# The last merge in two token passes with seven block products for eight, and its sums and output weights made ahead

## The chip, the core and the metric

The kernel runs on one core of one Trainium2 chip. The metric is the device time of one execution in microseconds (us). The engines are TensorE (PE: matrix products; PEld is its weight load), VectorE (DVE), ScalarE (ACT), GpSimd (POOL) and SyncE (SP, here an issuer of DMA transfers). All run side by side and meet through semaphores.

## The reference, cut to what matters

One step of a backbone layer for 2048 sample tokens and 128 prompt tokens, width 1024. Behind an adaptive RMSNorm one projection gives everything else:

```python
proj = einsum('btd,de->bte', xn, w_in)
qkv, beta, dec, z_a, u_b, v_b, z_b, x_c, z_c, gates = split(proj, points)
...                                  # three branches: DeltaNet scan, spatial gating, Fourier
br = stack([o_a, o_b, o_c], axis=2)                        # 3 branches, 512 wide
pb = einsum('btnw,nwd->btnd', br, w_branch)                # to 1024 channels each
gt = sigmoid(gates.reshape(B, T, 3, D_MODEL))              # 3 gates of 1024 channels
merged = einsum('btnd,btnd->btd', gt, pb)
out = einsum('btd,de->bte', merged, w_out)                 # then gated residual and RMSNorm
```

The gates are the largest product: 3072 of the projection's columns over all 2176 tokens.

## The kernel before, in words

**Numbers.** Every fp32 operand is kept as a pair of fp16 tiles, high part and low part, behind a power of two as scale. A product is then three matmuls for each 128 rows of depth: high by high, high by low, low by high. All go through the helper `mm` at L250, so the profile has one PE line. Depth 1024 takes 24 matmuls, depth 512 takes 12. The normed input lies in SBUF as `xh` and `xl` (1024 channels in 8 rows of tiles, by 2176 tokens). It stays until the gates are done. Weights arrive in fp32 (`wst`), are squared on ScalarE to find a scale (L315), and are turned into `whi` on ScalarE (L327) and `wlo` on VectorE (L328). For branch weights the names are `bst`/`wst`, `bhi` and `blo`.

**Order of stages.** Norm and small projections come first. Then q, k, v follow in 12 blocks of 128 channels (L927 to L956). Each block runs on PE over five token tiles (four of 512, one of 128). ScalarE moves each tile from PSUM to `raw` (L944), VectorE does the three-tap convolution over `raw` (L947 to L949), ScalarE and GpSimd the SiLU (L952, L953), and GpSimd stores the block (L954). `raw` has two buffers. Beside it a generator `decays()` computes the decay tables of the scan on VectorE and ScalarE, a few instructions for each token tile. After that come the rest of the projection, the branches and the scan.

**Merges.** `merge(n)` (from L1702) does one branch n: for each of 8 output blocks `db` and each token tile it makes the gate product (24 matmuls), a sigmoid on ScalarE (L1733), the branch product (12 matmuls), a multiplication on VectorE (L1742), and an addition on GpSimd into `mrow` (L1743). `mrow` is loaded from and stored to the DRAM rows `mD` (named `mrg`; L1717, L1758). The order is branch 1, 2, 0. In a merge's last block the next branch is loaded (`st` from `br`) and turned into the fp16 tile `big` (L1699, L1700). Weights of the next block are loaded and converted a block ahead (`weight_step`).

**Output weights and token sums of the output stage.** Merge 0 is the last. In its first four blocks it also makes the output weights (`out_w`: pairs `wohi`/`wolo` in SBUF, and four weight sums to DRAM as `tD`, named `tw`). In blocks 4 to 7 it adds, for each token tile, the four-way sums of merged rows that the output product takes (`quarters`, L1878 to L1887), and GpSimd stores them in DRAM as `paD` (named `pa`).

**Output stage.** It multiplies two token tiles at a time with seven block products where plain blocking takes eight (`two_tiles`; 84 matmuls of 512 columns each time, eight times). It starts with `prompt_left` (24 matmuls). Its inputs come through SP in one fixed order: rows of the prompt, `pa` of the first pair, weight sums `tw`, input rows, `pa` of the second pair. The large tiles of this stage lie on memory that has been used: `xh` and `xl` carry the input rows (`room`), the first pair's sums (`own`) and two of the weight sums; the others lie in a pool `opa` opened after `ms_.close()`.

**Who orders the work.** The code is written by stage, and a tile scheduler orders the instructions on each engine. Each engine then executes in that order. A tile that takes memory of a closed pool waits for the last users of what lay there.

## Time and profile before

| | |
|---|---|
| runs: median (lowest to highest), 3 runs | 2144.0 us (2141.62 to 2144.39) |
| profiled execution: span from first to last instruction | 2142.8 us |
| q, k, v blocks | about 145 to 422 us |
| merges 1, 2 and 0 | about 1050 to 1975 us |
| of these merge 0, the last | 1707.8 to 1975.1 us |
| output stage | 1975.1 us to the end |

The profiled execution's own time is its span; what a run has around it is not recorded apart, and the span lies 1.2 us under the median of the runs. In the profile's rows "L250" is the line of the program, "b<-xh,whi" says that PSUM bank b is written from the tiles xh and whi, "128x512" is the moving tile, and "x4" says that four like instructions are merged in one row. In a timeline the last part in brackets is the idle time of the engine before the row and what ended it. "SPq" and "POOLq" are rows in which SP or GpSimd issues a DMA.

### The profile page before, as it was taken

The page shows a single profiled execution, that of the slowest core. Times are in us where ns is not written, and L with a number is a line of the kernel's source. Part 1 is how long each engine was busy: PE and PEld are TensorE (multiplying, and loading weights), DVE is VectorE, ACT ScalarE, POOL GpSimd, SP SyncE. Part 2 cuts the span into 40 slices and gives each one's busy share as a digit, 9 for nine tenths or more (in the row PEclk, how much of TensorE's full clock was granted, in tenths as well). Part 3 has the DMA queues.
Part 4 walks back from the last instruction along what each step waited for, and adds up shares of the span by engine and source line. Part 5 has one row for each costly group of instructions (what it writes and reads, how often), then busy time and mean ns, then how long its engine had stood idle before and what let it go on. Part 6 is the DMA issues. An engine that isn't in the chain of part 4 may idle for free.

```text
span 2142.8 us, 42632 instructions
## 1 busy us (share of the span) xinstructions
PE 2084.4 (97%) x16133; PEld 1197.6 (56%) x16133; DVE 1330.7 (62%) x2945; ACT 1060.6 (49%) x2456; POOL 843.1 (39%) x1089
## 2 busy tenths in 40 slices
PE   8999999999999999999899999999999999999998
PEld 4454444455555677777555556565655444444443
DVE  6656854378777786566655555866665564666245
ACT  5554744465656664445544445665654353443112
POOL 0321332225565554552322233355543234343464
PEclk9999999999999999999999999999999999999999
DMA  9625722177877743444665556867664645456862
GB/s 352 222 78 191 266 103 103 62 222 234 262 226 240 228 143 99 121 132 141 204 182 166 164 160 188 262 211 226 211 198 128 210 169 173 167 197 234 344 221 89
DMA packets 222766, 403.25 MB, mean 188 GB/s; under 512 B 39704, under 2 KB 109616, under 8 KB 219744
## 3 DMA queue, kind: packets, MB, share of 16 engines
q1 hardware_dynamic: 167520, 290.58, 42.5%
q0 software_dynamic: 15216, 65.89, 8.2%
q10 hardware_dynamic: 39824, 44.05, 6.0%
q8 instruction: 127, 2.08, 0.4%
q14 instruction: 79, 0.65, 0.1%
HBM read 258.19 MB, written 142.24 MB: 187 GB/s over the span
## 4 chain that ended last, share of the span: by engine, by line
PE 50%; DVE 8%; DMA 7%; POOL 3%; ACT 3%; issue 3%; SPq 1%; ACTq 0%; POOLq 0%; DVEq 0%
PE b L250 49%; DMA st<-br 3%; POOL E L1115 1%; DMA pa<-pa 1%; DVE XB L1114 1%; POOL st L1466 1%; DVE big L1700 1%; DMA ei<-XB 1%; ACT big L1699 1%; ACT nd L1066 0%; DVE n L1083 0%; POOL ss L1024 0%; DVE XB L1123 0%; DMA br<-st 0%; DMA skn<-kv 0%
## 5 line engine op out<-in xcount | busy, mean ns | idle before, releaser
L250 PE MATMUL b<-xh,whi 128*128 128x512 f16 (+1 forms) x1920 | 650.3, 347 | 2.9 <-DVE sg L1456 1.8
L250 PE MATMUL b<-xl,whi 128*128 128x512 f16 (+1 forms) x1920 | 650.6, 347 | 0.0
L250 PE MATMUL b<-xh,wlo 128*128 128x512 f16 (+1 forms) x1920 | 649.7, 347 | 0.0
L250 PEld LDWEIGHTS <-whi 128*128 128x128 f16 x3856 | 352.4, 98 | 326.1 <-issue 6.9
L250 PEld LDWEIGHTS <-wlo 128*128 128x128 f16 x1928 | 188.6, 98 | 175.6 <-issue 1.2
L250 PE MATMUL b<-big,bhi 128*128 128x512 f16 (+1 forms) x960 | 253.2, 348 | 2.8 <-ACT big L1699 1.5
L250 PE MATMUL b<-big,blo 128*128 128x512 f16 (+1 forms) x480 | 163.4, 347 | 0.0
L1743 POOL TENSOR_TENSOR mrow<-mrow,sg 128x512 f32<-128x512 f32 (+1 forms) x80 | 94.4, 1183 | 129.4 <-DVE sg L1742 98.6
L953 POOL TENSOR_TENSOR cy<-cy,raw 128x545 f32<-128x545 f32 (+1 forms) x48 | 64.5, 1372 | 182.1 <-ACT raw L952 182.1
L250 PEld LDWEIGHTS <-xh 128*128 128x128 f16 x1496 | 117.1, 98 | 28.7 <-issue 1.3
L250 PEld LDWEIGHTS <-bhi 128*128 128x128 f16 x960 | 87.8, 98 | 79.2 <-issue 4.0
L1115 POOL TENSOR_TENSOR E<-E,XB 128x31 f32<-128x31 f32 (+15 forms) x155 | 94.3, 608 | 83.8 <-DVE XB L1114 67.6
L250 PEld LDWEIGHTS <-xl 128*128 128x128 f16 x1068 | 98.1, 98 | 44.8 <-DMA tw<-tw 1.3
L1733 ACT ACTIVATE sg<-b,winv 128x512 f32<-128x512 f32 (+1 forms) x120 | 74.0, 616 | 86.3 <-PE b L250 85.5
L1188 POOL COPY T<-ES 32x256 f16<-32x256 f16 x68 | 30.0, 442 | 182.9 <-DMA ES<-ei 159.6
L250 PE MATMUL b<-whi,xh 128*128 128x128 f16 x544 | 92.8, 219 | 0.0
L250 PE MATMUL b<-whi,xl 128*128 128x128 f16 x544 | 92.8, 219 | 0.0
L250 PE MATMUL b<-wlo,xh 128*128 128x128 f16 x544 | 92.8, 219 | 0.0
L328 DVE SCALAR_TENSOR_TENSOR wlo<-wst,wsc,whi 128x1024 f16<-128x1024 f32 x52 | 69.9, 1345 | 31.8 <-ACT whi L327 30.5
L315 ACT ACTIVATE wlo<-wst 128x1024 f16<-128x1024 f32 x52 | 54.9, 1055 | 53.0 <-DMA wst<-in_w_blk_dram 50.3
L1295 POOL TENSOR_TENSOR skn<-skn,ed 128x512 f32<-128x512 f32 x34 | 37.0, 1089 | 110.5 <-DMA skn<-kv 110.5
L1114 DVE TENSOR_TENSOR XB<-XB,E 128x31 f32<-128x31 f32 (+15 forms) x155 | 54.3, 350 | 42.0 <-POOL E L1115 41.3
(531 smaller groups left out, 4328.9 us busy)
## 6 DMA issues: line engine op xcount, KB each, us to landing
wst<-in_w_blk_dram SPq DMA_DIRECT2D x58, 512.0 KB, 4.5
pa<-pa POOLq DMA_DIRECT2D x16, 896.0 KB, 4.6
qkv<-cy POOLq DMA_DIRECT2D x12, 1089.0 KB, 5.3
st<-br SPq DMA_DIRECT2D x48, 256.0 KB, 3.3
mrow<-mrg SPq DMA_DIRECT2D x16, 576.0 KB, 4.7
pa<-pa SPq DMA_DIRECT2D x5, 1792.0 KB, 17.1
dc<-dec SPq DMA_DIRECT2D x17, 512.0 KB, 4.6
kq<-qkv SPq DMA_DIRECT2D x34, 256.0 KB, 4.3
```

The costliest lines, as they stand in the source:

```text
L250: newest[0] = PE.matmul(out, l, r, start=start, stop=stop, skip_group_check=reopened)
L315: w.squared = A.activation(w.lo, st, AF.Square, accum_out=ss)
L328: w.low = V.scalar_tensor_tensor(w.lo, st, s, w.hi, ALU.mult, ALU.subtract)
L953: G.tensor_tensor(y[:, c0:c1], y[:, c0:c1], raw[:, 1 + c0:1 + c1], ALU.mult)
L1114: V.tensor_tensor(t3, X3[:, 0:k, k:k + 1].to_broadcast([P, k, n_]), E3[:, k:k + 1, k:32].to_broadcast([P, k, n_]), ALU.mult)
L1115: G.tensor_tensor(E3[:, 0:k, k:32], E3[:, 0:k, k:32], t3, ALU.subtract)
L1188: G.tensor_copy(T16[rows(a0, b), :, :, b], ES[0:32, :, 2 * a0 + b, :, wT])
L1295: G.tensor_tensor(h3(kn_), h3(kn_), bc(ed[:, d, t, :], P), ALU.mult)
L1466: G.tensor_tensor(o, sg, src, ALU.mult)
L1699: A.activation(o16[:, 0, g, t0:t0 + tn], st, AF.Copy, scale=s)
L1733: gated_[0] = A.activation(sg, ps, AF.Sigmoid, scale=gw.inv)
L1743: G.tensor_tensor(mr, mr, sg, ALU.add)
```

## The change

**Seven products.** The last merge no longer goes through `merge`. `last_merge` takes a pair of gate blocks (i and i + 4), and cuts the tokens and the depth in halves a and b: tokens 0 to 511 with 512 to 1023, and so on (`QUADS`). Of the 2 by 2 by 2 small products it makes seven, on sums of token halves and sums of weight quarters, in place of eight. It runs over order (pass 1 with blocks 0 to 3, then pass 0): pass 1 takes tokens 1024 to 2047 and the 128 prompt tokens (as a small quad of 64 and 64), pass 0 tokens 0 to 1023. Branch products stay as many as before. The weights of each pair are loaded, added and converted in both passes (`pair_weights`); the scales of the first pass are kept.

**Sums ahead.** The sums of token halves (`token_sums`) and the output weights (`out_w`) are made as a generator `beside`, three steps behind each 512-token tile of q, k, v from block 1 on: 132 steps, just as many as there are places for. Results go to DRAM (`sD`, `woD`, `tD`). At the last block of merge 2 the sums are loaded again: three of the four into tiles `ts` of a new pool `last`, the fourth over the second token halves of `xh`/`xl`. After pass 1 the output weights are loaded into columns 1024 to 2047 of `xh`/`xl`, and the prompt's merged rows into the last 128 columns.

**Memory.** `mrow` and its neighbour `bwp` get a pool of their own (`mr_`) that is closed behind merge 2; a pool `orp` is opened on this memory with the new tiles of the last merge (`wt2`, `bst`, `bhi`, `blo`, `mr`, `pm`, `pa`, `sums`). The tiles of the output stage (`room`, three `pa`, `gpr`, `xr`) are moved to `opa`, opened behind `ms_.close()` and `last_s.close()`, on memory of `big`, `orp` and `last`. All four `tw` now go to columns 0 to 1023 of `xh`/`xl`.

**Small things.** `gates` (the rows of the residual gate) are advanced in every block of merge 2 and finished there; `dynamic_dma_scratch_size` is set to 4096.

Around the start of the last merge, PE before: behind the last product of merge 2 (bank b_23145) and two short sums stands the first gate product of merge 0 (b_23228), with weights made a block earlier.

```order
L250 MATMUL b_23145<-big_13436,blo_22675 128x128
L250 LDWEIGHTS ones_2_89
L250 MATMUL b_23201<-bsums_2759_23199,ones_2_89 128x27
L250 MATMUL b_23220<-sg_22571,sel_106 2x256 x2
L250 LDWEIGHTS whi_22891
L250 MATMUL b_23228<-xh_94,whi_22891 128x512
L250 LDWEIGHTS whi_22891
L250 MATMUL b_23228<-xl_95,whi_22891 128x512
```

The same place on PE after. The first row is again merge 2's last product.

```order
L251 MATMUL b_23758<-big_14010,blo_23330 128x128
L251 LDWEIGHTS ones_2_89
L251 MATMUL b_23817<-bsums_2925_23815,ones_2_89 128x27
L251 LDWEIGHTS ones_2_89
L251 MATMUL b_23847<-wscb_23845,ones_2_89 128x1
L251 LDWEIGHTS bhi_23873
L251 MATMUL b_24045<-big_14010,bhi_23873 128x512
L251 LDWEIGHTS bhi_23873
L251 MATMUL b_24045<-big_14010,bhi_23873 128x512
```

Where gate products with finished weights stood, there is now the sum for the scale of the first pair's weights (`wscb`), and behind it a branch product whose weights `bhi_23873` come of `bst`.

ScalarE there, after: `big` is the next branch's tile, and the rows L1987 are the squares of the first pair's weights, written to `wt` (the tile `wt2` of pool `orp`).

```order
L1785 ACTIVATE big_14010<-st_23729,bsc_23500 128x512
L1987 ACTIVATE wt_2933_23841,wss_2934_23842<-wst_23834 128x1024
L1785 ACTIVATE big_14010<-st_23775,bsc_23500 128x512
L1785 ACTIVATE big_14010<-st_23783,bsc_23500 128x128
L1987 ACTIVATE wt_2933_23841,wss_2934_23842<-wst_23835 128x1024
L1785 ACTIVATE big_14010<-st_23785,bsc_23500 128x128
L934 ACTIVATE bhi_23873<-bst_23838,bscale_23827 128x512
L934 ACTIVATE bhi_23877<-bst_23838,bscale_23827 128x512
L934 ACTIVATE whi_23853<-wst_23834,gscale_23832 128x512
```

The first of the rows L1987 waits for the last store of `mrow` to `mrg` in merge 2, since `wt2` lies where `mrow` lay; so does SP's load of `bst_23838`.

SP at the start of the output stage, before: `xh` and `xl` take the prompt's rows, the first pair and two weight sums.

```order
L1965 DMA xh_94<-in_x_prompt_dram 128x512
L1965 DMA xl_95<-pa 128x4x1792
L1965 DMA xl_95<-tw 128x4096 x2
L1965 DMA tw_3065_25690<-tw 128x4096
L1965 DMA xh_94<-in_x_sample_dram 128x1024 x2
L1965 DMA tw_3065_25690<-tw 128x4096
L1965 DMA pa_25703<-pa 128x4x1792
```

And after:

```order
L2162 DMA sg_26259<-gate 128x512
L2182 DMA room_26274<-in_x_prompt_dram 128x512
L2182 DMA pa_3208_26283<-pa 128x4x1792
L2182 DMA xh_94<-tw 128x4x1024 x2
L2182 DMA xl_95<-tw 128x4x1024
L2182 DMA room_26274<-in_x_sample_dram 128x1024 x2
L2182 DMA xl_95<-tw 128x4x1024
L2182 DMA pa_3209_26291<-pa 128x4x1792
```

The transfers and their order are nearly the same. The first waited for PE's last read of `xh` and `xl`. Now `room` waits for the last store of sums to `pa`, since it lies on memory of pool `orp`, and the rest is queued behind it.

The diff, cut to its core (the bodies of `token_sums`, `out_w` and `pair_weights` are shortened):

```diff
+QUADS = [(0, 512, 512, 0), (1024, 1536, 512, 512), (2048, 2112, 64, 1024)]
...
     for i, (n_, g) in enumerate(_blocks()):
+        if n_ == C_G:
+            break
...
+    def token_sums():
+        for p_, (a0, b0, cn, _) in enumerate(QUADS):
+            a, b = slice(a0, a0 + cn), slice(b0, b0 + cn)
+            for k in range(4):
+                f11, f12, f21, f22 = [sb(ep, [P, cn], "sg", bufs=4) for _ in range(4)]
+                for on, f, kk, ts in ((G, f21, k, b), (V, f11, k, a), (G, f22, k + 4, b), (G, f12, k + 4, a)):
+                    on.tensor_tensor(f, xh[:, kk, ts], xl[:, kk, ts], ALU.add)
...
+                for i, f in enumerate((f22, f11, f21, f12)):
+                    st = sb(ep, [P, 2, cn], "st", F16, bufs=3)
+                    as_pair(st[:, 0], st[:, 1], f, 1.0)
+                    SY.dma_start(sD[p_][:, i, :, k, :], st)
+                    yield 1
...
+                if tn == 512 and ct:
+                    for _ in range(3):
+                        next(beside, 0)
...
+    ms_, mr_ = ExitStack(), ExitStack()
     big = pool(ms_, "big", 1)
-    mrp = pool(ms_, "mrp", 2)
+    bwp.append(pool(mr_, "bwp", 1))
+    mrp = pool(mr_, "mrp", 2)
...
     inv_ = merge(2, False, inv_, finish_delta, then=(0, 17), step=norm_step)
+    mr_.close()
+    orp = pool(ms_, "orp", 1)
...
+            bst = sb(orp, [P, 2, 4, P], "bst")
+            t2 = sb(orp, [P, 4, P], "wt2")
...
+                    junk = t2.rearrange("p k c -> p (k c)").bitcast(F16).rearrange("p (k c) -> p k c", k=KT)
+                    A.activation(junk, st, AF.Square, accum_out=ss[:, n_:n_ + 1])
...
+        multiply(R, w.b11, ((0, a), (0, c)), True, 0)
+        multiply(Y, w.t2, None, True, 1, 1)
+        multiply(R, w.b21, ((4, a), (4, c)), False, 2)
+        multiply(Y, w.t3, None, False, 3, 2)
+        multiply(X, w.t1, ((0, b), (0, d)), True, 4)
+        m1a = gated(0, a, c11)
+        multiply(Y, w.t4, ((4, b), (4, d)), False, 5)
+        m2b = gated(1, b, u3)
+        multiply(X, w.b22, None, False, 6, 3)
+        m1b = gated(0, b, p1)
+        quarters(i, b0, m1b, m2b)
+        m2a = gated(1, a, u2)
+        quarters(i, a0, m1a, m2a)
...
+    order = [(1, i) for i in range(4)] + [(0, i) for i in range(4)]
-    merge(0, False, inv_, tail, HALVES[::-1], ahead_out, step=out_step)
     ms_.close()
+    last_s.close()
     opa = pool(ctx, "opa", 1)
-    room = xh.rearrange("p k t -> p (k t)").bitcast(F32)
+    room = sb(opa, [P, 8 * D + 512], "room")
```

403 lines of the change are left out of this document (280 added, 123 removed).

## The prediction

> **What bounds the kernel now.** I read the page first, then the groups of the last merge by shape, then the windows by stage, and last the timelines at both ends of the last merge. The page:
>
> ```profile
> span 2142.8 us, 42632 instructions
> PE 2084.4 (97%) x16133; PEld 1197.6 (56%) x16133; DVE 1330.7 (62%) x2945; ACT 1060.6 (49%) x2456; POOL 843.1 (39%) x1089
> ...
> PE 50%; DVE 8%; DMA 7%; POOL 3%; ACT 3%; issue 3%; SPq 1%; ACTq 0%; POOLq 0%; DVEq 0%
> ```
>
> TensorE is busy for 97% of the span, so time falls only where matmuls go, and rises wherever PE comes to wait. The last merge's products by shape (count, then busy us and mean ns):
>
> ```profile
> L250 PE MATMUL b<-xh,whi 128*128 128x512 f16 x256 | 97.0, 379 | 1.1 <-DVE sg L1742 1.1
> L250 PE MATMUL b<-big,bhi 128*128 128x512 f16 x256 | 76.1, 379 | 0.0
> L250 PE MATMUL b<-big,blo 128*128 128x512 f16 x128 | 48.5, 379 | 0.0
> L250 PE MATMUL b<-xh,whi 128*128 128x128 f16 x64 | 11.1, 219 | 0.0
> ```
>
> The gate has three groups like the first and like the last: 768 matmuls on 512 tokens and 192 on 128. The branch has 384 on 512 tokens. The mean of 379 ns contains overlap; I price by the distance of starts below. The windows give PE, PEld, DVE, ACT and POOL busy, granted clock, DMA share and GB/s:
>
> ```profile
> 149.00:151.00 2.00, 1.10 (x41) 1.10 (x42) 0.00 (x1) 0.90 (x1) 0.00 (x0) 0.50 0.89 228
> 153.00:155.00 2.00, 2.00 (x9) 0.62 (x6) 1.04 (x5) 1.86 (x4) 0.00 (x0) 0.50 0.03 8
> 172.00:200.00 28.00, 28.00 (x168) 14.21 (x167) 19.24 (x18) 12.71 (x18) 1.33 (x2) 1.00 0.67 217
> 200.00:227.00 27.00, 27.00 (x145) 12.94 (x144) 27.00 (x25) 17.55 (x21) 10.73 (x10) 1.00 0.69 247
> 227.00:254.00 27.00, 27.00 (x146) 13.04 (x145) 22.63 (x20) 19.13 (x25) 11.25 (x13) 1.00 0.85 305
> 335.00:362.00 27.00, 27.00 (x147) 12.96 (x145) 12.05 (x18) 12.25 (x20) 9.25 (x12) 1.00 0.23 81
> 1707.00:1975.00 268.00, 267.21 (x1466) 129.55 (x1466) 158.90 (x356) 118.24 (x201) 105.02 (x115) 1.00 0.53 183
> 1980.00:1990.00 10.00, 10.00 (x48) 4.53 (x47) 3.40 (x5) 1.99 (x5) 2.86 (x3) 1.00 1.01 422
> 1990.00:2000.00 10.00, 8.85 (x41) 3.73 (x40) 2.48 (x4) 0.00 (x0) 5.46 (x5) 1.00 1.02 418
> ```
>
> In the last merge PE is busy for 267.21 of 268 us. In the q, k, v blocks PE is full, and VectorE is full too from 200 to 227 us. At the start of the output stage the DMA engines are full (1.01, 1.02) and PE begins to wait (8.85 of 10).
>
> **The change part by part.**
>
> *Products.* Two pieces of the timeline give the prices: 24 gate matmuls of 512 columns run from 1707.79 to 1712.97, and starts of 128 columns lie 0.056 us apart. In the third piece four matmuls of 64 columns take 0.12 us.
>
> ```profile
> 1704.30 0.22 PE L250 MATMUL b<-xh,wlo 128*128 128x128 f16 x1
> 1704.36 0.22 PE L250 MATMUL b<-xh,whi 128*128 128x128 f16 x1
> ...
> 1705.48 0.22 PE L250 MATMUL b<-big,blo 128*128 128x128 f16 x1
> ...
> 1707.79 0.38 PE L250 MATMUL b<-xh,whi 128*128 128x512 f16 x1 [1.12 <-DVE sg L1742]
> 1707.81 2.14 POOL L1743 TENSOR_TENSOR mrow<-mrow,sg 128x512 f32<-128x512 f32 x2 [8.04 <-DVE sg L1742]
> 1710.25 0.57 POOL L1758 DMA_DIRECT2D mrg<-mrow  x1 [0.30 <-POOL mrow L1743]
> 1712.97 0.59 PE L250 MATMUL b<-big,bhi 128*128 128x512 f16 x2
> ```
>
> ```profile
> 912.87 0.28 PE L250 MATMUL b<-ES,Q 128*128 128x64 f16 x4
> 912.99 1.06 PE L250 MATMUL b<-cf,Y 128*128 128x128 f16 x12
> ```
>
> So a 512-column matmul costs 5.18 / 24 = 0.216 us and a 64-column one 0.03 us. Seven products for eight takes away 768 / 8 = 96 of 512 columns: 96 x 0.216 = 20.7 us. The prompt changes from 192 x 0.056 = 10.8 us to 4 pairs x 7 x 12 = 336 x 0.03 = 10.1 us. Together **-21.4 us**, all on the path since PE is full.
>
> The Trainium skill, page "TensorE: Matmul & The Clock Gate", section "Back-to-back issue gap", speaks against this gain: it gives about 131 ns for each 512-column matmul in a sustained stream with weight loads. By that the 96 would be worth 12.6 us, and the sum 8 us later. This stream of loads and matmuls shows 216 ns, and the measurement decides.
>
> *Start of the last merge.* Before, PE goes from merge 2's last product (1705.48) to the first gate product (1707.79) with a short wait. After, PE needs the first pair's weights, whose squares are written to a tile on memory of `mrow`, and so wait for the last store of merge 2. This store is issued at 1710.25, for the additions of 2.14 us on GpSimd precede it. Its landing and what follows:
>
> ```profile
> mrg<-mrow POOLq DMA_DIRECT2D x12, 576.0 KB, 3.8
> wst<-in_w_brb_dram SPq DMA_DIRECT2D x24, 256.0 KB, 3.5
> pa<-pa POOLq DMA_DIRECT2D x16, 896.0 KB, 4.6
> ```
>
> ```profile
> L315 ACT ACTIVATE wlo<-wst 128x1024 f16<-128x1024 f32 x52 | 54.9, 1055 | 53.0 <-DMA wst<-in_w_blk_dram 50.3
> ```
>
> The store lands at 1710.25 + 3.8 = 1714.05. The branch weights `bst`, held by the same store, land 3.5 later at 1717.55. The two squares end by 1716.2, and the pieces of `big` between them add about 1 us. Then comes the conversion of `bhi`, about half a square of 1.06 us with its start, taken as 0.8: PE begins near 1718.4 in place of 1707.8, **+11 us**. Ends: +7, if the store lands early and only the squares count; +16, if the landing takes 4.6 as the larger one does and the load queues behind SP's others for as long again. Once PE runs, 12 to 21 branch products (0.216 each) cover the conversion of the gate weights. Queued behind SP's held load are `mr`, `pm` and the next pair's weights, needed a pair-pass (28 us) later, so they cost nothing unless the wait exceeds that. The waiting squares hold ScalarE's remaining pieces of `big`, the branch of the last token tiles, which pass 1 needs later than its first product.
>
> *Start of the output stage.* I call the end of merge 0's last product T (1974.87 + 0.38 = 1975.25). Before:
>
> ```profile
> 1969.88 0.37 SPq L1965 DMA_DIRECT2D xl<-pa  x1
> ...
> 1974.87 0.38 PE L250 MATMUL b<-big,blo 128*128 128x512 f16 x1
> ...
> 1975.35 0.75 DVE L1742 SCALAR_TENSOR_TENSOR sg<-b,binv,sg 128x512 f32<-128x512 f32 x1 [1.37 <-PE b L250]
> ...
> 1976.18 1.26 POOL L1743 TENSOR_TENSOR mrow<-mrow,sg 128x512 f32<-128x512 f32 x1 [0.42 <-DVE sg L1742]
> ...
> 1977.17 0.50 SPq L1965 DMA_DIRECT2D pa<-pa  x1
> ...
> 1980.05 0.38 PE L250 MATMUL b<-wohi,wlo 128*128 128x512 f16 x1
> ...
> 1980.26 0.38 PE L250 MATMUL b<-wohi,xl 128*128 128x512 f16 x1
> ...
> 1983.31 0.73 POOL L1887 DMA_DIRECT2D pa<-pa  x1
> ```
>
> ```profile
> 1999.88 0.39 PE L250 MATMUL b<-wohi,pa 128*128 128x512 f16 x1 [0.32 <-DMA pa<-pa]
> ```
>
> The first pair's sums were fetched from 1969.88, ahead of T, and its products began at T + 5.0, right behind `prompt_left`. The second pair began at 1999.88 = T + 24.6, when its sums had landed. After, `room` waits for the last store of sums, and all inputs wait behind it on SP. This store is issued at T + 8.1 by the same chain (product, VectorE, GpSimd, sums), and lands 4.6 later: T + 12.7. Then `room` and the first pair (256 and 1792 KB: 2.1 MB at 420 GB/s is 5.0, with some 2 of start from the 3.5 of a small load) land at T + 19.7. PE, done with `prompt_left` at T + 5.0, waits 14.7. One pair is 84 x 0.216 = 18.1, so the second could start at T + 37.8. By then prompt rows, first pair, four `tw` of 1 MB, input rows and second pair, 9.2 MB at 420 GB/s, have needed 21.9 + 2: T + 36.6, so it isn't late. Net: 37.8 - 24.6 = **+13 us**. Ends: +11 with a landing in 4.6, as the 896 KB have it; +16.5 with 10.4, which is all the time from 1969.88 to 1980.26 that the first pair had before. Later pairs are PE-bound in both.
>
> *Clock.* Between 149 and 151 us PE is idle for 0.9 of 2 us and the granted clock is 0.50, and it is still 0.50 from 153 to 155 with PE busy. After waits of 11 and 15 us I expect it low for some 4 us each: 2 us lost each time, **+4 us** (0 to 6). The same page's section "Part 1: The HAM clock gate" has about 3.4 us at half clock after an idle stretch, which would be 1.7 each, and the sum 0.6 lower; the row above is compatible, without showing where a stretch begins.
>
> *Work beside q, k, v.* Token sums and output weights bring VectorE 9 instructions of 0.75 us (as the 512-wide one at 1975.35) for each large group of sums; with the output weights it is some 80 us over 11 blocks, or 9 for each 27 us. From 200 to 254 VectorE was busy for 49.6 of 54 us, from 335 on for 12 of 27. In the window from 172 it has 8.8 us free and could begin. For about two windows the work doesn't fit, and then it does. What hides it: six PSUM banks and two `raw` buffers let the convolutions come late by about one block, and `decays()`, which fills VectorE there, isn't due. Ends: 0 (all taken up) to +14 (the 18 us of new work in the two full windows less the 4.4 free, not buffered at all). Near the lower end, as PE there shows no wait: **+3 us**. The additions on GpSimd and the conversions on ScalarE fall on engines busy for at most 11 and 19 of 27.
>
> *The rest.* Inside the new merge a bank is used again one product (2.6 us) after its copy or sum is due, behind conversions of 0.7 to 1.3 on the in-order VectorE: **+2** (-1 to +8; below nothing if the sigmoid waits of merge 0 are better spread). Second loading and converting of weights (6.3 MB at 183 GB/s of traffic beside PE, in the room that `out_w` leaves): nothing. `gates` moved to merge 2: VectorE is idle there a third of the time; nothing, or 1 if it meets a weight conversion. The smaller DMA scratch shows nowhere in a row: 0, up to +2.
>
> Sum: -21.4 + 11 + 13 + 4 + 3 + 2 = +11.6 on the span, 2154.4; with the 1.2 us by which the span lies under the runs' median, **2155.6 us**. For this case alone 2144 to 2168.
>
> **The rivals.**
>
> *The output stage doesn't wait (not slower).* If `room`'s wait ends with an earlier store, or SP's loads get ahead of it, the end costs nothing and its clock loss goes too: 2155.6 - 13 - 2 = 2140.6. It decides at the landing of the first pair: at T + 5 or earlier there is no loss. For: the sums of this pair are stored in pass 1, long before. Against: the order on SP. If the start is also free, 13 less: 2127.6, faster.
>
> *VectorE starves PE in q, k, v.* If convolutions fall behind by more than one block, `raw` isn't free, ScalarE can't empty PSUM, and PE stops for most of the 14 us above, or again when `out_w` with its 1024-wide conversions starts: some +15 in place of +3, 2167.6. For: 27.00 of 27 busy. Against: PE is never idle there now.
>
> *The new merge waits at each product.* Half of 56 products each waiting 0.5 us gives 14 in place of 2: 2168. For: POOL and VectorE each have about 20 of 28 us to do. Against: three banks and four `sg` tiles.
>
> *Seven products don't save.* If 64-column matmuls cost as much as 128 columns (0.056), the prompt costs 18.8 in place of 10.1: 2164. Against: the row at 912.87.
>
> **How the numbers follow.** Chances: forecast 0.52, no wait at the end alone 0.13, none at either end 0.10, VectorE 0.13, new merge 0.08, small products 0.04. About 0.2% (4 us) is what measurements of this kernel can tell from no change. Faster (under 2140): the second of these rivals whole, half of the first and a tail of 0.04 of the forecast, 0.20. Same (2140 to 2148): the other half, and 0.09 of the forecast, 0.15. Slower: 0.65. The range for 8 in 10 goes from 2134 to 2170.
>
> **What would show it.** In the changed profile: 96 fewer 512-column matmuls at 0.216; PE idle for about 11 us behind merge 2's last product, ended by the branch weights; SP's `room` issued about 12.7 us after the last gated product and PE idle until 20; granted clock 0.50 after both; no long waits of PE between 200 and 260. I am wrong if PE goes through either end of the last merge with waits under 5 us, or if waits inside q, k, v exceed those at the ends.

## The result, and the profile after

The changed kernel takes 2242.0 us (median of 4 runs, 2239.1 to 2245.2) where the kernel before takes 2144.2 in the same session (4 runs, 2141.6 to 2144.9). The ratio is 1.045, with a 95% interval of 1.043 to 1.047. It is slower by 98 us; the forecast was 2155.6, and the range ended at 2170. The sign was right and the size was not.

The page of the changed kernel, to be read beside the page of before:

```profile
span 2237.3 us, 43354 instructions
PE 2085.7 (93%) x16169; PEld 1192.7 (53%) x16169; DVE 1493.8 (67%) x3056; ACT 1115.0 (50%) x2545; POOL 978.7 (44%) x1170
...
PE 42%; DVE 10%; DMA 8%; issue 4%; ACT 4%; POOL 3%; SPq 0%; ACTq 0%; POOLq 0%; DVEq 0%
```

TensorE's busy time is all but unchanged (2084.4 before), though 20 us of products are gone. Its share fell from 97% to 93%: idle time came in. VectorE has 163 us more, GpSimd 136 more.

Where the 94.5 us of span come from is read off five points that both programs have: the last copy of a q, k, v bank by ScalarE, the first product row of merge 1 on VectorE, the last branch product of merge 2, the first 512-column product of the last merge, and the end of its last product.

| stage, us | before | after | difference | forecast |
|---|---|---|---|---|
| start to the end of q, k, v | 415.2 | 468.0 | +52.8 | +3 |
| from there to merge 1 | 634.8 | 647.3 | +12.5 | 0 |
| merges 1 and 2 | 655.5 | 668.3 | +12.8 | 0 to 1 |
| gap ahead of the last merge | 2.3 | 13.4 | +11.1 | +11 |
| last merge | 267.5 | 250.3 | -17.2 | -21.4 + 2 + 2 |
| output stage | 167.5 | 189.9 | +22.4 | +13 + 2 |

Two rows came as forecast, and the output stage cost 7 us more; the loss sits in the first row, and two smaller ones in rows that were taken for nothing. For the q, k, v stage the windows of the changed kernel (PE, PEld, DVE, ACT and POOL busy, clock, DMA share, GB/s):

```profile
172.00:200.00 28.00, 18.85 (x117) 10.22 (x115) 26.21 (x39) 12.22 (x22) 16.29 (x12) 0.88 0.43 139
200.00:227.00 27.00, 27.00 (x145) 12.97 (x144) 25.92 (x20) 14.99 (x21) 16.82 (x12) 1.00 0.43 147
227.00:254.00 27.00, 23.02 (x130) 11.12 (x128) 25.84 (x24) 17.35 (x22) 18.75 (x11) 1.00 0.87 301
254.00:281.00 27.00, 23.76 (x121) 10.99 (x119) 27.00 (x25) 18.82 (x26) 13.65 (x12) 0.94 0.77 235
281.00:308.00 27.00, 23.71 (x120) 11.15 (x121) 27.00 (x24) 13.56 (x21) 16.52 (x9) 0.87 0.68 247
308.00:335.00 27.00, 20.54 (x88) 8.76 (x86) 23.46 (x34) 17.48 (x30) 17.57 (x22) 0.87 0.65 224
362.00:389.00 27.00, 19.27 (x80) 8.25 (x79) 18.56 (x20) 17.06 (x29) 12.08 (x13) 0.81 0.52 178
```

Before, PE was busy for the whole of each of these. Now VectorE is full or nearly so from 172 to 335 us, PE has gaps in all but one of the windows, and the clock falls. Over the whole stage, first the kernel before, then the changed kernel:

```profile
145.00:422.00 277.00, 275.78 (x1732) 138.05 (x1728) 157.98 (x183) 140.74 (x203) 70.69 (x89) 0.99 0.42 146
```

```profile
145.00:475.00 330.00, 292.29 (x1734) 142.56 (x1731) 270.65 (x334) 190.85 (x301) 177.18 (x151) 0.94 0.55 187
```

The stage is 53 us longer. Of these, 330 - 292.3 less 277 - 275.8, or 36.5, is idle time of PE. The other 292.3 - 275.8 = 16.5 is for the most part a lower clock: 58 matmuls of 512 columns start some 0.42 us behind the one before with no wait between (7 before), in place of 0.216, which makes 10.6 us. Some 4 more are 18 further matmuls of 512 columns, work of the next stage that PE takes up before ScalarE has emptied the last bank of q, k, v. VectorE has 270.7 us of work where it had 158.0. What PE waited for in that stretch (us in total, times, longest):

```profile
PE b L251 <- DVE wlo L330: 17.0, 3, 6.5
PE b L251 <- DVE wscb L265: 7.7, 1, 7.7
PE b L251 <- DVE tok L871: 5.8, 1, 5.8
PE b L251 <- DVE oss2b L982: 2.9, 1, 2.9
PE b L890 <- DVE tok L879: 2.2, 1, 2.2
```

All are short pieces of work on VectorE: the low half of a weight block, the sum from which its scale is made, the decays' small tables. `oss2b` is the like sum for the output weights: the new work also puts four small products into PE's queue, and PE waits there for VectorE too. One of the low halves in VectorE's timeline, and what it stood behind:

```profile
240.56 1.63 DVE L960 TENSOR_TENSOR sg<-sg,sg 128x512 f32<-128x512 f32 x1
...
242.24 3.07 DVE L935 SCALAR_TENSOR_TENSOR st<-sg,st 128x512 f16<-128x512 f32 x2
...
247.39 1.64 DVE L954 TENSOR_TENSOR sg<-xh,xl 128x512 f32<-128x512 f16 x1
...
252.49 1.27 DVE L330 SCALAR_TENSOR_TENSOR wlo<-wst,wsc,whi 128x1024 f16<-128x1024 f32 x1
```

The high half of that weight block was ready on ScalarE at 244.5 (1.14 us from 243.40). VectorE, which takes its queue in order and was never idle, came to the low half at 252.5; PE had waited 3.98 us for it when it went on at 253.82. Between them stand token sums, decays and a convolution.

### The profile page after: what moved, and what is told of

Same layout as the page of the kernel before. It is cut to its first block, busy times and chain, and to the rows that moved or that the text cites. A ratio compares the mean times of both kernels' runs of the same rounds, so it can differ in the third digit from the quotient of the medians.

```text
span 2237.3 us, 43354 instructions
## 1 busy us (share of the span) xinstructions
PE 2085.7 (93%) x16169; PEld 1192.7 (53%) x16169; DVE 1493.8 (67%) x3056; ACT 1115.0 (50%) x2545; POOL 978.7 (44%) x1170
## 4 chain that ended last, share of the span: by engine, by line
PE 42%; DVE 10%; DMA 8%; issue 4%; ACT 4%; POOL 3%; SPq 0%; ACTq 0%; POOLq 0%; DVEq 0%
PE b L251 41%; DMA st<-br 2%; DMA wst<-in_w_blk_dram 1%; DMA wst<-in_w_ada_dram 1%; DVE pa L935 1%; DMA br<-o 1%; POOL E L1201 1%; DVE XB L1200 1%; DMA ei<-XB 1%; DVE wlo L935 1%; DMA pa<-pa 1%; DMA N<-n 1%; DVE wlo L330 0%; POOL mr L2080 0%; DVE big L1786 0%
## 5 line engine op out<-in xcount | busy, mean ns | idle before, releaser
L251 PE MATMUL b<-xh,wlo 128*128 128x512 f16 (+2 forms) x1792 | 599.8, 347 | 17.0 <-DVE wlo L330 17.0
L251 PE MATMUL b<-xh,whi 128*128 128x512 f16 (+2 forms) x1792 | 602.5, 347 | 6.6 <-ACT sg L2090 3.1
L251 PE MATMUL b<-xl,whi 128*128 128x512 f16 (+2 forms) x1792 | 603.0, 347 | 0.0
L251 PE MATMUL b<-xh,pa 128*128 128x512 f16 x376 | 100.7, 383 | 20.1 <-DMA pa<-pa 20.1
L251 PEld LDWEIGHTS <-pa 128*128 128x128 f16 x648 | 63.8, 99 | 98.4 <-issue 23.3
L1825 POOL TENSOR_TENSOR mrow<-mrow,sg 128x512 f32<-128x512 f32 (+1 forms) x40 | 48.4, 1210 | 83.0 <-DVE sg L1824 62.6
L251 PEld LDWEIGHTS <-xl 128*128 128x128 f16 x824 | 74.5, 98 | 14.4
L251 PE MATMUL b<-xl,pa 128*128 128x512 f16 x272 | 77.2, 382 | 0.0
```

What stands on the lines that cost most here:

```text
L251: newest[0] = PE.matmul(out, l, r, start=start, stop=stop, skip_group_check=reopened)
L1825: G.tensor_tensor(mr, mr, sg, ALU.add)
```

## The experiments

Times are medians, each against runs of the kernel before on the same chip (2144 to 2148).

### Which part costs

**The work beside q, k, v alone.** The kernel before plus the changed kernel's token sums and output weights, made beside q, k, v and not used, with the smaller DMA scratch:

```
+    beside = one_by_one(token_sums(), out_w2())
...
+                if tn == 512 and ct:
+                    for _ in range(3):
+                        next(beside, 0)
```

> The kernel before, with the token sums and the output weights made beside q, k, v as in the change, and nothing else of the change but the DMA scratch of 4096; their results go to DRAM and nobody reads them. Theory 1 (the work beside q, k, v makes VectorE late, and weight conversions with it): the last convolution ends about 50 us later than before, PE idles some 35 us between 145 and 475 us, and the whole is about 2194 to 2204. If the drift of 25 us in the scan and in merges 1 and 2 also comes of this work, about 2215 to 2225. Rival (the q, k, v loss comes of another part of the change, its memory or its DMA loads): q, k, v within 10 us of before, whole under 2155.

2214.5 us, ratio 1.032 (1.030 to 1.035). The end of q, k, v comes 53.9 us later than before, merge 1 70.4, and from merge 2's end on it is 68 to 70. So some 70 of the 98 us are this part, and nothing later in the kernel is needed for them.

**The gate rows alone.** The kernel before, with its gate rows advanced as in the changed kernel, in blocks 4 to 7 of merge 1 and in all of merge 2:

```
-                if each is not None and (n == 0 or db > 3):
+                if each is not None or db > 3:
```

> The kernel before with one line of the change: the rows of the residual gate are advanced in blocks 4 to 7 of merge 1 and in every block of merge 2, not in merge 2's second half and in merge 0. Theory (their loads share two buffers with the gate weights, and their two sums go through VectorE and PE, which costs merges 1 and 2 the 15 us that the changed kernel drifts there): about 2155 to 2160. Rival (the drift there comes of the order of instructions or of lateness carried over from before): 2140 to 2146.

2156.1 us, ratio 1.0054 (1.0034 to 1.0073). Merges 1 and 2 take 668.6 us in place of 655.5, as in the changed kernel (668.3); the last merge is 1.5 shorter. This part costs 10 to 12.

**The gate rows on buffers of their own.** The run above, with tiles apart from those of block weights and sigmoids, and with the smaller DMA scratch to make room:

```
-            acc = sb(ep, [P, 512], "sg", bufs=4)
+            acc = sb(gwp, [P, 512], "gacc")
...
-                st = sb(wp, [P, 4, 256], "wst", bufs=2)
+                st = sb(gwp, [P, 4, 256], "gst")
```

> The kernel before with its gate rows advanced as in the changed kernel (blocks 4 to 7 of merge 1 and all of merge 2; 2156.1), but with the gate weights and their running sums on three tiles of their own, not on the buffers of the block weights and sigmoids (and a smaller DMA scratch, to make room). If the shared buffers cost the 10 to 12 us, the time falls to 2144 to 2148. If VectorE's multiply-adds of the gate rows stand in the way of the delta steps that run beside the merges, it stays at 2153 to 2158.

2166.3 us, ratio 1.0083 (1.0054 to 1.0111), above both of my ranges. Merges 1 and 2 still take 668.1 us, though a quarter of the multiply-adds now runs earlier (merge 1 begins 7.8 us late). So the shared buffers are not the cause of the 12.6 us there. VectorE's queue is left. In the run with the gate rows alone, these are the 64 instructions (the last columns: its idle time ahead of them and for what):

```profile
L476 DVE SCALAR_TENSOR_TENSOR sg<-wst,scT,sg 128x256 f32<-128x256 f32 x56 | 26.4, 516 | 8.5 <-DMA wst<-in_w_ada_dram 8.4
L474 DVE TENSOR_SCALAR sg<-wst,scT 128x256 f32<-128x256 f32 x8 | 3.7, 480 | 5.6 <-DMA wst<-in_w_ada_dram 5.4 <-POOL o L1372 0.2
```

They take 30.1 us, and the queue stands for another 13.8 while their weights land. But it is not the amount: 32 of them stood in merge 2 before, from 1572 us on, and VectorE's busy time in the two merges goes only from 393.0 to 401.6 us, with own buffers to 395.8. What differs is the place. All 64 now lie between 1224 and 1541 us, among the steps of the delta rule, which pass through VectorE and ScalarE one after another. PE's waits in the two merges grow from 8.6 to 15.9 us, most of them for such steps, up to 2 us each. That a delay of this chain makes the 12.6 us is the reading that fits; it was not isolated.

### Why the work beside q, k, v costs 54 and not 3

**All of it on GpSimd.** The changed kernel with the additions and low halves of the token sums moved from VectorE:

```
-                V.tensor_tensor(f22, f21, f22, ALU.add)
+                G.tensor_tensor(f22, f21, f22, ALU.add)
...
-                    as_pair(st[:, 0], st[:, 1], f, 1.0)
+                    A.activation(st[:, 0], f, AF.Copy, scale=1.0)
+                    G.tensor_tensor(st[:, 1], f, st[:, 0], ALU.subtract)
```

> The changed kernel, with all additions of the token sums on GpSimd, and the low parts of their pairs too (a subtraction, as their scale is 1); ScalarE, the transfers and the output weights are as in the change. Theory 1 (VectorE is what is overloaded): VectorE loses some 75 us of work between 145 and 400 us, PE's waits for weight conversions there fall from 38 to under 12 us, and the whole falls by 25 to 45 us, to about 2195 to 2215. Rival (the waits come of engines waiting for each other in turn, or of ScalarE or the loads, and GpSimd becomes the slow one): within 10 us of 2242, or slower.

2273.3 us, ratio 1.059 (1.057 to 1.061): 31 slower still, as the rival had it. From 200 to 389 us:

```profile
200.00:389.00 189.00, 150.39 (x765) 69.94 (x763) 133.81 (x101) 96.37 (x146) 187.88 (x154) 0.91 0.50 176
```

```profile
PE b L251 <- ACT raw L1026: 31.8, 11, 13.1
PE b L251 <- DVE wscb L265: 16.0, 3, 10.0
```

VectorE has room now (133.8 of 189), and GpSimd is full (187.9). The gating products of the convolutions stand behind the sums in its queue, `raw` isn't freed, and ScalarE can't empty a bank: the path that the rival "VectorE starves PE" described, by way of GpSimd.

**Later, by steps, held, or behind the weights.** Four runs on the kernel with the added work alone: its steps traced from the fifth block on; the same from the second or from the fifth block on and each step held behind the copy of its tile's bank on ScalarE; and the weight conversions ahead of all else in the order:

```
-                if tn == 512 and ct:
-                    for _ in range(3):
+                if tn == 512 and ct > 3:
+                    for _ in range(4):
```

> The kernel before with the same work beside q, k, v as the run b_beside, but begun at block 4, four steps behind each tile, when the decay tables are nearly done. Theory 1 (VectorE is given more than it can do from 172 to 335 us, where the decay tables and the convolutions fill it already, and its in-order queue then holds the weight conversions): most of the 68 us of b_beside go, the end of q, k, v lies at most 20 us behind that of before, the whole at 2150 to 2175. Rival (whatever its place, each piece of this work holds PE by waits between engines and by stores in SP's queue): 2195 or more.

```
-                if tn == 512 and ct:
-                    for _ in range(3):
-                        next(beside, 0)
+                if tn == 512 and ct > 0:
+                    with tc.issue_after(moved.ins):
+                        for _ in range(3):
+                            next(beside, 0)
```

> As the run begun from the fifth block, but from the second block on, three steps for each token tile, so that the steps are spread over all blocks and don't run ahead of the work of their tile. Theory (amount in full windows): the first blocks stay overfull, so most of the loss stays: 2190 to 2212. Rival (what cost was the running ahead of conversions that PE needs, not the amount): at most 2165.

```
+                if tn == 512 and ct > 3:
+                    with tc.issue_after(moved.ins):
+                        for _ in range(4):
+                            next(beside, 0)
```

> The kernel before with the token sums and output weights beside q, k, v (2214.5 us when begun at once), but begun only from the fifth of the twelve blocks, four steps for each token tile, and each step's instructions put in the program behind the copy of the bank of the same tile, so that a good part of them comes after the decays, where VectorE was busy for 12 of 27 us. Theory (too much work for VectorE in windows that the decays already fill): the end of q, k, v comes less than 20 us later than in the kernel before instead of 54, and the time is at most 2175. Rival (the steps cost about the same wherever they stand, through the DMA queue, the conversions or the clock): the end is still 40 us late or more, and the time 2200 or more.

```
+        with hurry():
             sb16 = widened(ss, wp, "wsc")
...
+    rush[0] = True
```

> The kernel of b_beside, with the weight conversions of the q, k, v blocks put first among the instructions that the scheduler can choose from; work and place are the same. Theory 1 (PE waits because conversions stand behind sums and decay tables in VectorE's order): PE's waits for conversions between 145 and 475 us fall from 38 to under 15 us, the whole from 2214 to 2170 to 2190. Rival (VectorE has so much to do that PSUM and the raw buffers run full instead, or the weights are late by their loads): 2200 or more.

2211.1, 2213.0, 2215.6 and 2207.5 us: ratios 1.031, 1.031, 1.032 and 1.029, each within 0.003 either way. Three came out as their rivals had it, the second a microsecond above its theory's range. The first did not move the work, so it says nothing of the place: the scheduler puts instructions early when nothing holds them, and VectorE's windows from 172 to 335 us stayed as they were. The third did move it. PE is fully busy there from 172 to 254 us, and then:

```profile
281.00:308.00 27.00, 24.77 (x133) 11.89 (x132) 25.48 (x26) 11.60 (x22) 21.79 (x17) 1.00 0.36 130
308.00:335.00 27.00, 18.10 (x95) 8.48 (x94) 25.60 (x25) 11.46 (x20) 22.37 (x15) 0.87 0.35 129
335.00:362.00 27.00, 14.42 (x77) 6.77 (x76) 25.05 (x24) 11.64 (x20) 20.15 (x15) 0.75 0.41 146
362.00:389.00 27.00, 17.09 (x69) 7.14 (x68) 23.75 (x35) 13.52 (x26) 21.88 (x25) 0.81 0.38 130
```

The same loss, later: the stage ends 52.6 us late in place of 53.9, and my expectation for that run (under 20) fell. VectorE is as good as full in these windows, where in the kernel before it had 9.6 to 15.5 us of 27. By waiting, the work only found less time ahead of it. With the steps spread from the second block on, the stage ends 61 us late; 18.9 of PE's 43 us of waits there are for `oss2b`, so in a good part of that loss PE stands at the small products of the new work itself. Putting the weights first gained 7 us, and PE then waited for scales and the decays' tables.

**Without the low halves.** The work beside q, k, v, but only the high halves are made and stored, so what lies in DRAM is not the sums:

```
-                    as_pair2(st[:, 0], st[:, 1], f, 1.0)
-                    SY.dma_start(sD[p_][:, i, :, k, :], st)
+                    A.activation(st[:, 0], f, AF.Copy, scale=1.0)
+                    SY.dma_start(sD[p_][:, i, 0, k, :], st[:, 0])
```

> The kernel before with the work beside q, k, v (2214.5), but without VectorE's making of the low halves (78 instructions, 61 us in that run's profile): only the high halves are made and stored, so the sums and output weights kept in DRAM lack their low half. GpSimd's additions, the loads, the scale products on PE and the conversions on ScalarE stay. Theory (VectorE's whole load of some 270 us in a stage of 277 us): with about 205 us the end of q, k, v comes less than 15 us later than in the kernel before instead of 54, and the time is at most 2165. Rival (the loads, GpSimd or the added scale products cost it): 30 us or more stay, 2180 or more.

**Without GpSimd's additions.** VectorE's instructions are as many, from other operands, so the sums are not those wanted:

```
-                    on.tensor_tensor(f, xh[:, kk, ts], xl[:, kk, ts], ALU.add)
+                V.tensor_tensor(f11, xh[:, k, a], xl[:, k, a], ALU.add)
...
-                V.tensor_tensor(f22, f21, f22, ALU.add)
-                G.tensor_tensor(f21, f11, f21, ALU.subtract)
+                V.tensor_tensor(f22, f11, f11, ALU.add)
```

> The same work without GpSimd's additions: VectorE has as many instructions of the same shapes, but makes them from its own sums and the weights as they are, so what is kept in DRAM is not the sums wanted. If VectorE's instructions are stretched by GpSimd working beside it (convolution 2.85 us in place of 2.49, a low half 0.96), they shorten towards those of the kernel before, VectorE's load falls to some 235 us, and the end of q, k, v comes 15 to 30 us late; time 2160 to 2185. If the instruction count alone matters, 45 us or more stay and the time is 2200 or more.

2185.3 us (1.0165, 1.0142 to 1.0187) and 2179.1 (1.0135, 1.0109 to 1.0162). The stage ends 36.0 and 27.8 us late, where the whole work has 53.9. The first run missed its theory's bound of 15 us, and its rival's (30 or more) held; the second fell in its range. So neither is the cause alone: of 54 us, taking away 61 us of VectorE's work gives back 18, and taking away GpSimd's additions, with not one instruction less on VectorE, gives back 26. Nor is it VectorE's sum alone. From 145 us to the end of q, k, v it is busy for 264 us with the whole work, 212 without low halves and 225 without GpSimd's additions, and the run with 212 ends later than the one with 225. In both VectorE is still full (27.00 of 27) for the windows from 200 to 254 us, without low halves to 281, and PE loses time there.

The second run changes two things, which these runs don't part. The steps no longer pass from VectorE to GpSimd and back, and VectorE's own instructions get shorter. First the kernel before, then the work alone, then without GpSimd's additions (us in all, mean ns):

```profile
L949 DVE SCALAR_TENSOR_TENSOR cy<-raw,pc,cy 128x2178 f32<-128x2178 f32 x11 | 27.3, 2485 | 0.6
```

```profile
L1030 DVE SCALAR_TENSOR_TENSOR cy<-raw,pc,cy 128x2178 f32<-128x2178 f32 x11 | 31.3, 2845 | 0.0
L932 DVE SCALAR_TENSOR_TENSOR st<-sg,st 128x512 f16<-128x512 f32 x32 | 30.3, 961 | 1.9 <-ACT st L931 1.8
```

```profile
L1027 DVE SCALAR_TENSOR_TENSOR cy<-raw,pc,cy 128x2178 f32<-128x2178 f32 x12 | 29.8, 2480 | 0.2
L932 DVE SCALAR_TENSOR_TENSOR st<-sg,st 128x512 f16<-128x512 f32 x32 | 23.4, 742 | 3.0 <-ACT st L931 2.9
```

A low half takes 961 ns beside GpSimd and 742 without, and a convolution step with two tensors 2845 in place of 2485. These are means of two cases, as the changed kernel's timeline shows:

```profile
261.74 2.19 POOL L957 TENSOR_TENSOR sg<-sg,sg 128x512 f32<-128x512 f32 x1 [5.23 <-DVE sg L956]
262.72 3.49 DVE L1033 SCALAR_TENSOR_TENSOR cy<-raw,pc,cy 128x2178 f32<-128x2178 f32 x1
...
297.34 2.47 DVE L1033 SCALAR_TENSOR_TENSOR cy<-raw,pc,cy 128x2178 f32<-128x2178 f32 x1
297.56 2.42 POOL L954 TENSOR_TENSOR sg<-xh,xl 128x64 f32<-128x64 f16 x1 [3.63 <-DVE sg L959]
```

Where GpSimd's addition started first, the step takes about a microsecond more (3.37 to 3.49 us in 6 of the 24 such steps); where VectorE started first it takes its 2.47, and by its row GpSimd's 64-column addition lasts until the step is over. Of the 32 low halves with 512 columns, 12 have an addition of GpSimd ahead of them and take 1.15 to 1.64 us; the other 20 take 0.67 to 0.69, three of them with GpSimd beside them. The step with one tensor does the same: 1.34 to 1.36 us, or 2.24 to 2.27 in the 3 of 12 where GpSimd was ahead. What loss stays in the run without GpSimd's additions is for the most part one wait of 14.5 us, for a bank that ScalarE could not empty:

```profile
PE b L251 <- ACT raw L1019: 14.5, 1, 14.5
```

**Elsewhere.** The changed kernel with three edits told of below (2212.4), and the sums and output weights made in the merges, on 12 KB of their own; then the same with each step held behind its token tile's gated product on VectorE and sigmoid on ScalarE:

```
-    tp = pool(a1, "tp", 1, side="right")
+    tp = pool(mr_, "tp", 1)
...
+                    if tn == 512 and (first or db < 4):
+                        for _ in range(3):
+                            next(beside, 0)
```

> The changed kernel with the earlier three edits (2212.4), and the token sums and output weights made in merges 1 and 2 in place of q, k, v, on 12 KB of their own. The end of q, k, v should be that of the kernel before, 415, within 2 us. If VectorE's idle third of the merges takes the work up, the time is 2144 to 2150; if it costs the delta steps there a quarter of its 110 us, as the gate rows' some 45 us seem to cost 10 to 12, 2165 to 2180.

```
+                    if tn == 512:
+                        with tc.issue_after(held.ins), tc.issue_after(gated_[0].ins):
+                            for _ in range(3 if first else 2):
+                                next(beside, 0)
```

> As the run that made the sums and output weights in the merges (2234.7; there they were issued early all the same, between 817 and 977 us, in the scan before the merges), but with each step held behind the gated product of its own token tile on VectorE and behind its sigmoid on ScalarE, so that they really stand spread over merges 1 and 2. With the kernel before's 1050 us at the start of merge 1, and a loss of 20 to 30 us in the merges (their delta steps pass through VectorE too; 10 to 13 us for the gate rows' 16 rounds of 8 instructions), the time is 2160 to 2180. If VectorE's idle third of the merges takes the work up without loss, 2144 to 2150. If work of this size costs 65 us in any stage, 2205 or more.

2234.7 us (1.0395, 1.0374 to 1.0417) and 2197.2 (1.0247, 1.0214 to 1.0280). In the first, q, k, v end at 415.8 as before, so what else this kernel has of the change costs no time there, the smaller DMA scratch included. But the time is above both of my ranges: nothing held the sums in the merges, most of them ran from 817 to 977 us, in the scan, and merge 1 began 71 us late. In the scan PE waited once for 33 us on a GpSimd instruction of the delta rule:

```profile
PE b L251 <- POOL T L1203: 33.4, 1, 33.4
```

In the second they stand in the merges, whose length grows by 39 us to 694.6, and merge 1 begins 11.5 late, with GpSimd's first additions still early. That is 15 better than beside q, k, v, between the range that I expected (2160 to 2180) and the bound for "any stage" (2205); VectorE there is busy for 487 of 720 us. So spreading helps, but this work was hidden in none of the three places.

### The ends of the last merge

**Memory for the start.** The changed kernel with the tiles that shared memory with `mrow` moved:

```
-            bst = sb(orp, [P, 2, 4, P], "bst")
+            bst = sb(last_[0], [P, 2, 4, P], "bst")
...
-            t2 = sb(orp, [P, 4, P], "wt2")
+            t2 = sb(last_[0], [P, 4, P], "wt2")
```

> The changed kernel with four kinds of tiles of the last merge (the squares' target, the branch weights as loaded, and their two fp16 parts) in the pool that is opened at the last block of merge 2 on memory of the scan, so that none of them lies where merge 2's rows lay. Theory (PE's wait at the start of the last merge is for the last store of merge 2, through this memory): the wait of 12.2 + 0.8 us falls to under 3, the whole by 10 to 13 us, to 2229 to 2232. Rival (the weights would be late anyway, by their loads and conversions): a wait of 8 us or more stays, and the whole falls by under 5.

2241.1 us (1.0445, 1.0427 to 1.0464), no change, as the rival had it for the time. The gap falls from 13.4 to 7.3 us, but the merge takes 257.6 in place of 250.3, most of it one wait of 7.1 us on `msc`, the next thing due.

**The first weights early.** The first pair's weights converted in merge 2's last block, in a pool of their own:

```
+            last_.append(pool(pw_s, "pw", 1, side="right"))
...
+    cur = pair_weights(0, False)
...
+        if db == KT - 1:
+            cur.upto(next(made_))
```

> The changed kernel (2242.0) with the first pair's weights of the last merge converted inside merge 2's last block, on a pool of their own, and nothing else. If the wait at the start of the last merge is a true cost of 11 us, the time falls to about 2231; if work that the start no longer has room for comes back as waits inside the merge, as the run with three edits suggests (start 1.9 us, merge 264.0 in place of 250.3), gap and merge together stay at 263 to 266 and the time within 3 us of 2242.

2241.0 us (1.0445, 1.0412 to 1.0478), no change in time. In the profile the gap is 2.8 and the merge 253.6, together 7.3 less; merge 1 begins 5.5 later, and merges 1 and 2 take 672.6, 4.3 more. This edit touches nothing ahead of merge 1, and the next run, which changes nothing ahead of the output stage, has 672.4 us for merges 1 and 2, so neither is put down to the edit. The time came as expected, gap and merge did not: the gain at the start is there in part, and differences of its size between programs, ahead of it, hide it.

**The output's first pair.** Its sums loaded onto memory that is free earlier, ahead of `room`:

```
+    own = [sums[j, 0].rearrange("p l k c -> p (l k c)")[:, 0:3584]
...
+        if i == 0:
+            ready.append(own)
```

> The changed kernel with the first pair of the output stage on memory of two of the token sums, which the last pair of gate blocks has done with some 15 us before its end; it and the four weight sums are loaded ahead of what lies on the other pools' memory. Theory (PE's 20 us at the start of the output stage are a wait for memory and for SP's order, not for the transfers): the wait at the first pair falls from 20 to under 3 us, up to 5 come at the second pair, and the whole falls by 14 to 21 us, to 2221 to 2228. Rival (the transfers themselves need that time): falls by under 7.

2230.3 us (1.0388, 1.0365 to 1.0410), 12 less, a little short of the 14 to 21 expected; the output stage takes 174.7 in place of 189.9. Its wait of 20 us is gone, and one of 3.3 has come.

**Three edits, and with the held work.** Output and early weights as above, gate rows back to merge 2 and the last merge; then the same with the work beside q, k, v held from the fifth block on:

```
-                if each is not None or db > 3:
+                if each is not None and db > 3:
```

> The changed kernel with three mends: the end as in a_end; the gate rows where they were, in merge 2's second half and in the last merge; the first pair of gate weights converted during merge 2's last block, on memory of its own. The work beside q, k, v is untouched. By the runs so far: end -14 to -21, gate rows -10 to -14, start -9 to -13, so about 2195 to 2209. If the mends hide in one another or the new merge's weights come late, above 2215.

```
+                if tn == 512 and ct > 3:
+                    with tc.issue_after(moved.ins):
```

> The changed kernel with the earlier three edits (output start, gates back, first weights early: 2212.4) and the work beside q, k, v held behind each tile's copy from the fifth block on. If holding takes away 35 to 50 of the 54 us lost by the end of q, k, v, this gives 2160 to 2178, still slower than 2144 before; if it takes away all 68 that this part cost, 2144. If holding does nothing, 2212.

2212.4 us (1.0311, 1.0288 to 1.0334) and 2216.0 (1.0320, 1.0297 to 1.0344). Merges 1 and 2 are back at 653.6 us and the gap at 1.9, but the last merge takes 264.0: the gate rows now run in it, and its waits are

```profile
PE b L251 <- ACT sg L2095: 6.1, 5, 2.5
PE b L251 <- DVE st L2043: 6.0, 4, 3.5
```

for sigmoids and sums, where in the kernel before it waited 1.1 us in all. With three of the four costs mended, what remains of the loss, 67 us, is about what the work beside q, k, v costs alone. Holding that work gained nothing more. No version here beats the kernel before.

## Why the prediction was wrong, point by point

**Work beside q, k, v: the step that failed.** The prediction put it at "+3 us", ends 0 to +14. It measured +53 at the end of the stage, and about +70 with what follows. The steps of its working that failed:

- *The amount.* "9 instructions of 0.75 us", some 80 us in all, became 113. The kernel has 8 for each large group, four additions and four low halves, not 9; the 96 instructions of 512 columns took 91 us, 0.95 each, and those of 64 columns for the prompt 12 more. The price came from a 512-wide instruction in the last merge. Beside GpSimd's additions low halves take 0.96 and the additions 0.80 to 1.40, and the convolutions already there are stretched as well.
- *The fit.* "For about two windows the work doesn't fit, and then it does." It was full or nearly so for six windows, from 172 to 335 us, and PE lost time in five of them. VectorE's sum for the stage is 158.0 + 112.7 = 270.7 us in a stage of 277, 98%; I had it at hand as 158 + 80 = 238 and looked only at the two fullest windows. The sum is a warning and not the whole cause: with 212 us, 77%, the stage still ended 36 us late.
- *What fails first.* The prediction weighed how late a convolution may be. Most waits are for something else in the same queue: the weight blocks' low halves and scales, a few us before PE needs them. Two `raw` buffers are no cover for these.
- *GpSimd's and ScalarE's share "fall on engines busy for at most 11 and 19 of 27".* An engine that is half idle was not free: without GpSimd's additions 26 of the 54 us are gone.
- *The clock.* I charged half clock only at the ends of the last merge. Here it is some 11 us.

The rival "VectorE starves PE in q, k, v" (0.13, at 2168) names the right engine and place; its price of +15 was the 14 of the ends, with the same arithmetic. The Trainium skill, page "SBUF — State Buffer", section "Who interferes with whom", says that a VectorE instruction with two SBUF inputs contends with a GpSimd instruction that reads SBUF, the loser being blocked, and that one with at most one SBUF input doesn't, outside the 2-port perf modes, which `tensor_scalar` can enter. The rows with two tensors agree: 2485 to 2845 ns and 742 to 961. The step with one tensor was slowed as well, 1.34 to 2.24 us where GpSimd was ahead; no row tells whether it ran in such a mode. That section of the Trainium skill spoke against this change, and I did not weigh it.

**From q, k, v to merge 1: not in the sum.** +12.5 us in the changed kernel, 16.5 with the work alone, 4.4 without the low halves and 7.8 without GpSimd's additions. But the gate rows on own buffers, without this work, have 7.8 as well, and edits far behind this stretch moved it by -1.4 to +5.8. Which waits make it up is not settled.

**Gate rows: "nothing, or 1".** +12.8, by the run with that edit alone 10 to 12 on the time. That VectorE is idle there for more than a third of the time was true and beside the point. What failed is "nothing"; the reading that fits is the chain of the delta rule, which passes through its queue, and that the runs leave open.

**Start of the last merge: +11, measured +11.1.** The links are as told:

```profile
1783.62 0.22 PE L251 MATMUL b<-big,blo 128*128 128x128 f16 x1
...
1787.80 0.57 POOL L1835 DMA_DIRECT2D mrg<-mrow  x1 [0.30 <-POOL mrow L1825]
...
1792.66 1.06 ACT L1987 ACTIVATE wt<-wst 128x1024 f16<-128x1024 f32 x1 [1.28 <-DMA mrg<-mrow]
...
1796.99 1.86 PE L251 MATMUL b<-big,bhi 128*128 128x512 f16 x4 [0.82 <-DMA mr<-mrg]
```

The store is issued 4.2 us behind merge 2's last product, the square starts when it has landed, and PE starts 4.3 later. The experiments add that this wait is not a cost that can be lifted by itself: with the memory moved, it fell by 6.1 us and the merge took 7.3 longer.

**Products and inner waits: -21.4 + 2 + 2, measured -17.2.** Right in size. In the last merge the groups of 512-column gate matmuls come to 128 three times, 192 and 96, or 672 in place of 768, at the same 379 ns, and PE is idle for 4.4 of 250 us in it (before 0.8 of 268). The 131 ns for a 512-column matmul that the Trainium skill gives (page "TensorE: Matmul & The Clock Gate", section "Back-to-back issue gap") would have made the merge 8 us longer than the rows of before did; it came out by the rows.

**Start of the output: +13 + 2, measured +22.4.** The mechanism was right and the size short. With T = 2047.3:

```profile
2052.45 0.74 DVE L935 SCALAR_TENSOR_TENSOR pa<-mr,msc,pa 128x512 f16<-128x512 f32 x1
...
2058.88 0.73 POOL L1929 DMA_DIRECT2D pa<-pa  x1 [4.53 <-DVE pa L935]
2063.37 0.33 SPq L2182 DMA_DIRECT2D room<-in_x_prompt_dram  x1
2063.75 0.43 SPq L2182 DMA_DIRECT2D pa<-pa  x1
...
2072.58 0.59 PE L251 MATMUL b<-xh,pa 128*128 128x512 f16 x1 [20.08 <-DMA pa<-pa]
```

The last store of sums leaves at T + 11.6, not T + 8.1, behind the sums and halves of the last two token tiles on VectorE. It lands after 4.5 as put. Then `room` and the pair take 9.2 in place of 7. PE goes on at T + 25.3 where T + 19.7 was put, and for that it pays again at a clock of 0.76:

```profile
2062.00:2072.00 10.00, 0.00 (x0) 0.00 (x0) 0.00 (x0) 0.72 (x2) 1.25 (x1) 0.50 0.79 283
2072.00:2082.00 10.00, 9.42 (x35) 3.82 (x36) 0.69 (x1) 0.59 (x1) 0.00 (x0) 0.76 1.04 393
```

**The rivals at the ends.** The output did wait. Small products did save: 64-column matmuls stand 0.029 us apart in the new merge. And the new merge waited 5.2 us inside, in place of the 14 of its rival.

## What to carry to other kernels

Before work is put beside a stage, add up the whole stage for each engine that it touches, the old work and the new: at 98% of VectorE, in order, it wasn't hidden. A lower sum is no promise either: at 77% 36 us were lost, in windows that were full. An idle share on an engine is cover only if nothing urgent passes through its queue; look for short instructions that TensorE waits for (scales, low halves, steps of a chain) and count what will stand ahead of them. And an instruction is priced in the company that it will have: 0.74 us without GpSimd's additions became 0.96 beside them, as the mean of those that GpSimd had started ahead of and those that it hadn't.

## What the hardware showed

Half clock costs more in many short waits than in one long one. In the changed kernel's q, k, v stage PE resumes after 5.8 us:

```profile
178.47 1.68 PE L251 MATMUL b<-tok,cst 128*128 128x68 f32 x6 [5.79 <-DVE tok L871]
179.94 0.63 PE L251 MATMUL b<-xl,whi 128*128 128x512 f16 x1
180.37 0.63 PE L251 MATMUL b<-xh,wlo 128*128 128x512 f16 x1
...
182.46 0.38 PE L251 MATMUL b<-xl,whi 128*128 128x512 f16 x1
182.67 0.38 PE L251 MATMUL b<-xh,wlo 128*128 128x512 f16 x1
```

512-column matmuls stand 0.43 us apart up to about 182, 0.21 after: half speed for some 4 us, 2 us lost, which is what I had put for one wait. A wait of 5.8 us thus costs 7.8, and the stage's waits cost some 11 us on top of the 37 that they last. The one wait of 20.1 us at the output's start costs little more than one of these: the 10 us behind it ran at 0.76, which is 2.4 lost. (The Trainium skill, page "TensorE: Matmul & The Clock Gate", section "Part 1: The HAM clock gate", gives a window of about 3.4 us; from 178.47 to 182.46 are 4.0.)
